# Values and decayed keys turned to tokens by 32x32 blocks on VectorE, with the blocks placed by GpSimd, in a hybrid RWKV-7 step

## The chip, the cores and the metric

The kernel runs on one core of a Trainium2 chip. A core has a matrix engine (TensorE, in the profile PE for its products and PEld for the loading of its stationary operand), VectorE (DVE), ScalarE (ACT), GpSimd (POOL), and queues that issue transfers (SP's is the one used here almost alone). Each engine works through its own list of instructions in order, and waits at the head of the list when an operand is not ready. The metric is the device time of one execution in microseconds (us). The kernel before took 2240.18 us (median of three runs, 2237.89 to 2241.36).

## What is computed

One layer of a bidirectional RWKV-7 mixer beside a gated convolution, on 384 tokens (128 of context, 256 latent) with 2048 channels in 32 heads of 64. The part that matters here is the scan, which runs in both directions d:

```python
def step(S, inp):
    r_t, w_t, k_t, v_t, a_t, b_t = inp
    sa = jnp.einsum('dbhij,dbhj->dbhi', S, a_t)
    S = S * w_t[..., None, :] + sa[..., :, None] * b_t[..., None, :] + v_t[..., :, None] * k_t[..., None, :]
    y = jnp.einsum('dbhij,dbhj->dbhi', S, r_t)
    return S, y
...
y_a = (y.astype(h.dtype) * jax.nn.silu(g_a)) @ w_out_a
...
return merged @ w_o, S_fin
```

All else is large projections: `z = h @ w_in` with 20864 columns, three output projections, and elementwise work. All is float32; the projections are computed as three products of split halves (a high part, rounded to the matrix engine's format, and the low part that is left).

## The kernel before, in words

Channels lie on the 128 partitions and tokens along a row, so that a block of 128 channels holds two heads. There are 16 blocks (`b` from 0 to 15). The scan is done in chunks of 64 tokens, `NCH` = 6 per direction.

Two kinds of work share the matrix engine, whose order is written out by hand. The first is the **stream** (`Stream`, L111): projections against weights that come in as `raw` tiles, are split into `whi` by ScalarE (L88) and `wlo` (the low part) by VectorE (L89), and are multiplied in units of three products (`mm3`, L81 to L83). `ds_.go(n)` puts n units into the engine's order. The second is the scan of the blocks, in whose gaps the units stand. Per block, in this order:

- `prep_b`: VectorE forms `bk` (L672, L673: for each chunk the 64 columns of b and the 64 columns of k, both undecayed) and `pr` (L674 to L679). Then come 14 units (`PB0`), `finish` of the block before (the matrix engine turns `ytok`, L931, after VectorE's L925, which waits for GpSimd's `rs`, L924), and for each direction the products `pA` (L700), masked into `A` by VectorE (L706), with 6 units (`PB1`) behind each. GpSimd scales `bk` by the chunk's decay (L713), as soon as the products have read it. The diagonal 32x32 corners of `A` go through memory (L710, L716) to the tile `U`, and VectorE inverts them all in a chain of 60 dependent steps (L721 and L723 in turn, in whose gaps the scheduler places other work of VectorE, such as L89). ScalarE turns the result (L727), and transfers take it back into `A` and into `x11` (L728 to L735; the profile calls that tile x).
- `prep_c`: the values `v` (and `vr`, a copy of `v` read backwards) and the scaled `bk` are turned from channels to tokens by the matrix engine, three or four 128x128 turns into a PSUM bank at a time (L761, L770), and copied out by ScalarE into the lower half of `sav` (L763) and into `bt` (L771). Then `pav` (L776) multiplies `A` with `sav`, and GpSimd clears a part of `A` (L783).
- `drive` and `go` fill up to 80 units (`WINDOW`), in which `prep_a` of the next block runs; then `scan` begins with the products `pH` (L852), which read `x11`, and goes on to `pq` (L831, reads `A` and `sav`), `pu` (L838, reads `bt`) and `po`.
- `norm`: mean, variance and scale of `ytok` (L915 to L925).

The order on VectorE, ScalarE, GpSimd and SP is the scheduler's; the order on the matrix engine is the program's own. `tmp` takes one of eight buffers in turn.

Of the kernel before, what the change touches and what calls it, by code (L numbers as in the profile page):

```python
# [9 lines left out]
F32 = mybir.dt.float32  # L10
# [5 lines left out]
P = 128  # L16
# [5 lines left out]
C = 64  # L22
NCH = 6
# [33 lines left out]
def hybrid_step(ctx, tc, cst, x_prompt, x_sample, state_f, state_b, c, c_ctx, ada_w, ada_b, norm_g,  # L57
# [3 lines left out]
    V, S, G, TE = nc.vector, nc.scalar, nc.gpsimd, nc.tensor  # L61
# [14 lines left out]
    ident = cs[:, C_ID:C_ID + P]  # L76
# [176 lines left out]
    def pcol(i, n=1):  # L253
        return par[:, i:i + n]
# [151 lines left out]
    r_, k_, v_, ga_ = {}, {}, {}, {}  # L406
    box = {}

    def tmp(nm):
        return box["sp"].tile([P, T], F32, tag="t", name=nm, bufs=8)  # L410
# [134 lines left out]
    sp = ctx_sc.enter_context(tc.tile_pool(name="sp", bufs=1))  # L545
# [6 lines left out]
    for i in range(3):  # L552
        t = tmp(f"lst_{i}")
# [4 lines left out]
    for m in range(4):  # L558
# [6 lines left out]
        t = tmp(f"lin_{m}")  # L565
# [3 lines left out]
        src = t[0:96, ::-1] if m % 2 else t[0:96, :]  # L569
# [20 lines left out]
    def bank(nm):  # L590
        return ps1.tile([P, 4, P], F32, tag="A", name=nm, bufs=5)
# [4 lines left out]
    def flat(a):  # L596
        return a.rearrange("p n t -> p (n t)")
# [4 lines left out]
    def hl_parts(t, hi, nm):  # L602
        lo = sp.tile([P, T], F32R, tag="t", name=f"lo_{nm}", bufs=8)
        S.copy(hi[:], t[:])
        V.tensor_tensor(lo[:], t[:], hi[:].bitcast(F32), ALU.subtract)
        return hi, lo
# [56 lines left out]

    def prep_b(b, o):

        r, kk = r_[b], o["kk"]
        o["pr"], o["bk"] = [], []
        for d in range(2):
            ep, em, kd, bn = o["ep"][d], o["em"][d], o["kd"][d], o["bn"][d]
            pr = sp.tile([P, NCH, P], F32, tag=f"pr{d}", name=f"pr_{b}_{d}")  # L670
            bk = sp.tile([P, NCH, P], F32, tag=f"bk{d}", name=f"bk_{b}_{d}")
# [20 lines left out]
        A = sp.tile([P, 2, 2 * NCH, P], F32, tag="A", name=f"A_{b}")  # L692
        o["A"] = A
        for d in range(2):
            pr, bk = o["pr"][d], o["bk"][d]
# [15 lines left out]

        for d in range(2):
            G.tensor_tensor(o["bk"][d][:], o["bk"][d][:], o["ep"][d][:, :, C:C + 1].broadcast_to([P, NCH, P]), ALU.mult)  # L713

        U = sp.tile([48, 32, 32], F32, tag="U", name=f"U_{b}")
        nc.sync.dma_start(U[:], ui[:].rearrange("d e i s t -> (d e i) s t"))  # L716
# [19 lines left out]

    def prep_c(b, o):

        r, v, A = r_[b], v_[b], o["A"]

        s_in = sp.tile([P, 2, C], F32, tag="s_in", name=f"s_in_{b}")
        for d in range(2):
            for h in range(2):
                for jb in range(2):
                    p0 = C * h + 32 * jb
                    nc.sync.dma_start(s_in[p0:p0 + 32, d, :].rearrange("i (b j) -> i b j", j=32),
                                      ctx_st[d][0, 0, 2 * b + h].rearrange("(b i) j -> i b j", i=32)
                                      [:, :, 32 * jb:32 * jb + 32])

        sav = sp.tile([P, 2 * NCH, P], F32, tag="sav", name=f"sav_{b}")  # L750
        bt = sp.tile([P, 2 * NCH, P], F32, tag="bt", name=f"bt_{b}")
        o["sav"], o["bkt"] = sav, bt
        for d in range(2):
            if d == 0:
                src = v
            else:
                src = tmp(f"vr_{b}")
                S.copy(src[:], v[:, ::-1])
            pv = bank(f"pv_{b}_{d}")
            for q in range(3):  # L760
                TE.transpose(pv[:, q, :], src[:, q * P:(q + 1) * P], ident)  # L761
            for e in range(2):
                S.copy(sav[C:P, NCH * d + e:NCH * d + NCH:2, :], pv[C * e:C * e + C, 0:3, :])  # L763
            yield 1
        for d in range(2):

            for n0, n1 in (((0, 4), (4, 5)), ((0, 3), (4, 6)))[d]:
                pb = bank(f"pb_{b}_{d}_{n0}")
                for n in range(n0, n1):
                    TE.transpose(pb[:, n - n0, :], o["bk"][d][:, n, :], ident)  # L770
                S.copy(bt[:, NCH * d + n0:NCH * d + n1, :], pb[:, 0:n1 - n0, :])  # L771
                yield 1
        pvs = [bank(f"pav_{b}_{d}") for d in range(2)]
        for f in range(2 * NCH):
            for h in range(2):
                TE.matmul(flat(pvs[f // NCH][hss[h]])[:, C * (f % NCH):C * (f % NCH) + C], A[C:P, 0, f, hss[h]],  # L776
                          sav[C:P, f, hss[h]], start=True, stop=True)
        for d in range(2):
            for h in range(2):
                S.copy(sav[0:C, NCH * d:NCH * d + NCH, hss[h]],  # L780
                       flat(pvs[d][hss[h]])[:, 0:NCH * C].rearrange("p (n i) -> p n i", i=C))

        G.memset(A[C:P, 0, :, :], 0.0)  # L783
        yield 2
        ks = o["kd"]
        V.tensor_tensor(ks[0][:], ks[0][:], ks[1][:, ::-1], ALU.add)
        V.scalar_tensor_tensor(ks[0][:], ks[0][:], pcol(RK + b), r[:], ALU.mult, ALU.mult)
        o["bsum"] = hl_parts(ks[0], sp.tile([P, T], F32R, tag="t", name=f"bsh_{b}", bufs=8), f"bs_{b}")
        yield 1
        for h in range(2):  # L790
            for d in range(2):
                V.transpose(st[1][hss[h], d, hss[h]], s_in[hss[h], d, :])
# [145 lines left out]
    def drive(gen, prio=0, at=None, fn=None):  # L938
        n = i = 0
        while True:  # L940
            if i == at:
                fn()
            i += 1
            with tc.high_priority(offset=prio):
                u = next(gen, None)
            if u is None:
                return n
            ds_.go(u)
            n += u
# [6 lines left out]
    for b in range(NB):  # L956
        if b < NB - 1:
            if b > 0:
                ds_.urgent += [(add_rk, b + 1), (add_gv, b)]
        if b == NB - 2:  # L960
            ds_.fills += [(add_gv, NB - 1)] + [(add_ob, g) for g in range(8)]
        pb_gen = prep_b(b, cur)
        ds_.go(next(pb_gen))
        if prev is not None:
            finish(b - 1, prev)
        drive(pb_gen)
        n = drive(prep_c(b, cur))
        nxt = {}
        if b < NB - 1:
            while f"gv{b}" not in ds_.done:  # L970
                ds_.go(1)
                n += 1
            n += drive(prep_a(b + 1, nxt))
        w = WINDOW + (FIRST if b == 0 else LAST if b == NB - 1 else 0)
        if n < w:
            ds_.go(w - n)

        def keys():

# [128 lines left out]
    for half in range(2):  # L1108
# [8 lines left out]
        for s in range(3):  # L1117
# [10 lines left out]
            if half == 1:  # L1128
                f = rsf[:, s, :]
# [37 lines left out]
```

## Time and profile before

| | |
|---|---|
| median of 3 runs | 2240.18 us |
| the profiled execution | 2242.0 us |
| its span, first to last instruction | 2240.2 us |
| mean granted clock of the matrix engine | 0.996 |
| ACT busy | 1044.3 us (47%) |
| POOL busy | 116.5 us, 113 instructions |
| GpSimd's scaling of `bk` (L713) | 32 times, 50.2 us |
| turns of `bk` on PE (L770) | 160, 27.9 us busy |
| turns of `v` and `vr` on PE (L761) | 96 |
| ScalarE's copies into `sav` behind them (L763) | 64, 30.2 us |

The blocks run from about 185 us to 1890 us; block 3, which the prediction works through, has its products `pA` at 521.67 and 526.55 us. The time of a product counts from its start to its modelled end, and the next one starts before that, so the distance between starts tells what a product takes from the engine. Times in a timeline are from the start of the span: start, duration, engine, line, operation, tiles, count, and in brackets the idle time before and what ended it.

### The profile page before, as it was taken

To read this page: it belongs to the slowest core of one execution; us is meant where nothing else is said; L and a number is where in the kernel's file an instruction comes from. 1 tells how busy PE (TensorE), PEld (TensorE's weight loads), DVE (VectorE), ACT (ScalarE), POOL (GpSimd) and SP (SyncE) were. 2 spreads that over 40 slices of the span, in tenths; PEclk is the share of its full clock that TensorE was granted. 3 is DMA by queue.
4 is the path that set the end of the run, shared out by engine and by line. 5 is a ranking of instruction groups with operands and counts; after the bars stand their busy time and mean duration, and the time that the engine had idled before them with its cause. 6 is when DMAs were issued, how large, how long until landed. Compare 5 with 4: busy or idle time off the path is not lost.

```text
span 2240.2 us, 40545 instructions
## 1 busy us (share of the span) xinstructions
PE 2179.2 (97%) x16020; PEld 2064.9 (92%) x16020; DVE 1540.2 (69%) x3208; ACT 1044.3 (47%) x1800; POOL 116.5 (5%) x113
## 2 busy tenths in 40 slices
PE   5899999999999999999999999999999999999998
PEld 3588999999999999999999999999999999998988
DVE  3248567787777778777878787777777774444354
ACT  4245445454545454454545454546455543333333
POOL 2000010101010100000010101010100000000000
PEclk9999999999999999999999999999999999999999
DMA  9973544444444445443444434444445455886633
GB/s 335 346 211 116 147 129 133 111 120 125 112 125 120 113 117 132 115 132 103 124 109 133 111 110 134 112 118 140 120 121 143 146 179 162 292 281 230 221 132 113
DMA packets 440397, 339.97 MB, mean 152 GB/s; under 512 B 95552, under 2 KB 421776, under 8 KB 439312
## 3 DMA queue, kind: packets, MB, share of 16 engines
q1 hardware_dynamic: 438720, 335.63, 51.1%
q8 instruction: 126, 2.06, 0.4%
q10 hardware_dynamic: 432, 1.57, 0.2%
q14 instruction: 63, 0.52, 0.1%
q0 software_dynamic: 1056, 0.19, 0.1%
HBM read 307.37 MB, written 29.36 MB: 150 GB/s over the span
## 4 chain that ended last, share of the span: by engine, by line
PE 81%; DVE 8%; DMA 5%; ACT 3%; SPq 2%; issue 1%; POOL 0%; POOLq 0%; ACTq 0%; DVEq 0%
PE d_rk L81 4%; PE d_rk L83 4%; PE d_rk L82 4%; PE d_gv L81 3%; PE d_gv L82 3%; PE d_gv L83 3%; DMA raw_adah<-in_ada_w_dram 3%; PE pA L700 2%; PE d_oa L81 2%; PE d_oa L83 2%; PE d_oa L82 2%; PE d_bc L81 2%; PE d_mb L81 2%; PE d_bc L83 2%; PE d_bc L82 2%; PE d_bx L81 2%
## 5 line engine op out<-in xcount | busy, mean ns | idle before, releaser
L721 DVE TENSOR_TENSOR ut<-U 48x30 f32<-48x30 f32 (+14 forms) x480 | 154.6, 322 | 16.2 <-DMA U<-ui 4.1
L81 PE MATMUL d_rk<-h_hi,whi_rk 128*128 128x384 f32 x480 | 163.0, 340 | 0.6 <-ACT lst L554 0.6
L723 DVE TENSOR_TENSOR U<-U,ut 48x30 f32<-48x30 f32 (+14 forms) x480 | 154.5, 322 | 12.1
L81 PE MATMUL d_gv<-h_hi,whi_gv 128*128 128x384 f32 x480 | 161.0, 335 | 0.0
L83 PE MATMUL d_gv<-h_hi,wlo_gv 128*128 128x384 f32 x480 | 160.7, 335 | 0.0
L82 PE MATMUL d_gv<-h_lo,whi_gv 128*128 128x384 f32 x480 | 160.7, 335 | 0.0
L83 PE MATMUL d_rk<-h_hi,wlo_rk 128*128 128x384 f32 x480 | 160.4, 334 | 0.0
L82 PE MATMUL d_rk<-h_lo,whi_rk 128*128 128x384 f32 x480 | 160.4, 334 | 0.0
L88 ACT CAST whi_gv<-raw_gv 128x1024 fp32r<-128x1024 f32 (+1 forms) x64 | 64.0, 1000 | 139.6 <-PE d_rk L82 96.9
L88 ACT CAST whi_rk<-raw_rk 128x1024 fp32r<-128x1024 f32 x60 | 63.0, 1054 | 106.4 <-PE d_rk L82 31.7
L89 DVE TENSOR_TENSOR wlo_rk<-raw_rk,whi_rk 128x1024 fp32r<-128x1024 f32 x60 | 72.9, 1218 | 44.9 <-ACT whi_rk L88 39.7
L81 PE MATMUL d_gb<-h_hi,whi_gb 128*128 128x384 f32 x256 | 92.2, 360 | 0.0
L924 POOL TENSOR_TENSOR rs<-var,nhalf 128x6 f32<-128x6 f32 x16 | 21.2, 1325 | 1364.1 <-DVE var L922 1364.1
L81 PE MATMUL d_bc<-h_hi,whi_bc 128*128 128x384 f32 x256 | 92.2, 360 | 0.0
L81 PE MATMUL d_bg<-h_hi,whi_bg 128*128 128x384 f32 x256 | 92.1, 360 | 0.0
L81 PE MATMUL d_bx<-h_hi,whi_bx 128*128 128x384 f32 x256 | 92.1, 360 | 0.0
L81 PEld LDWEIGHTS d_rk<-h_hi,whi_rk 128*128 128x128 f32 x480 | 90.1, 188 | 1.8 <-ACT lst L554 0.9
L81 PE MATMUL d_ma<-h_hi,whi_ma 128*128 128x384 f32 x256 | 91.7, 358 | 0.0
L81 PE MATMUL d_ob<-ybh,whi_ob 128*128 128x384 f32 x256 | 88.9, 347 | 2.6 <-ACT whi_ob L88 2.1
L81 PEld LDWEIGHTS d_gv<-h_hi,whi_gv 128*128 128x128 f32 x480 | 90.5, 189 | 0.2
L82 PEld LDWEIGHTS d_gv<-h_lo,whi_gv 128*128 128x128 f32 x480 | 90.5, 188 | 0.0
L83 PEld LDWEIGHTS d_gv<-h_hi,wlo_gv 128*128 128x128 f32 x480 | 90.4, 188 | 0.0
(315 smaller groups left out, 6641.9 us busy)
## 6 DMA issues: line engine op xcount, KB each, us to landing
raw_adah<-in_ada_w_dram SPq DMA_DIRECT2D x64, 512.0 KB, 8.6
raw_rk<-in_w_in_dram SPq DMA_DIRECT2D x60, 512.0 KB, 5.3
raw_gv<-in_w_in_dram SPq DMA_DIRECT2D x60, 512.0 KB, 4.9
raw_ma<-in_w_in_dram SPq DMA_DIRECT2D x16, 1024.0 KB, 5.5
raw_mb<-in_w_in_dram SPq DMA_DIRECT2D x16, 1024.0 KB, 5.7
raw_bc<-in_w_in_dram SPq DMA_DIRECT2D x16, 1024.0 KB, 5.5
raw_bx<-in_w_in_dram SPq DMA_DIRECT2D x16, 1024.0 KB, 5.4
raw_bg<-in_w_in_dram SPq DMA_DIRECT2D x16, 1024.0 KB, 5.5
```

The costliest lines, as they stand in the source:

```text
L81: TE.matmul(out, wh, xh, start=start, stop=False)
L82: TE.matmul(out, wh, xl, start=False, stop=False)
L83: TE.matmul(out, wl, xh, start=False, stop=stop)
L88: S.copy(hi[0:rows], src)
L89: V.tensor_tensor(lo[0:rows], src, hi[0:rows].bitcast(F32), ALU.subtract)
L700: TE.matmul(pas[h, n // 4 * 4][:, n % 4, :], bk[hss[h], n, :], pr[hss[h], n, :], start=True, stop=True)
L721: V.tensor_tensor(tv, U[:, 0:s, s:s + 1].broadcast_to([48, s, w]), U[:, s:s + 1, s + 1:].broadcast_to([48, s, w]), ALU.mult)
L723: V.tensor_tensor(U[:, 0:s, s + 1:], U[:, 0:s, s + 1:], tv, ALU.add)
L924: G.tensor_tensor(rs[:], var[:], nhalf[:], ALU.pow)
```

## The change

The 16 turns per block on the matrix engine, the copy `vr` and ScalarE's copies out of PSUM are gone. Instead VectorE turns each 32x32 block in place within its own 32 partitions (`V.transpose`): `v` and `v` backwards at the start of `prep_b` into two temporary tiles `vt`, and each direction's scaled `bk` in place behind GpSimd's scaling. GpSimd then copies blocks from one group of 32 partitions to another: 16 copies of 32 x 192 elements into `sav`, and 32 of the same size into `bt`. The matrix engine no longer has units between the turns; since `go` fills up to the same window, these units stand later.

```diff
     def prep_b(b, o):
 
-        r, kk = r_[b], o["kk"]
+        r, kk, v = r_[b], o["kk"], v_[b]
+
+        sav = sp.tile([P, 2 * NCH, P], F32, tag="sav", name=f"sav_{b}")
+        o["sav"] = sav
+        for d in range(2):
+            x = tmp(f"vt_{b}_{d}")
+            V.transpose(x[:], v[:, ::-1] if d else v[:])
+            x = x[:].rearrange("p (n e t) -> p n e t", e=2, t=32)
+            for e in range(2):
+                for q in range(4):
+                    G.tensor_copy(sav[C + 32 * e:C + 32 * e + 32, NCH * d:NCH * d + NCH, 32 * q:32 * q + 32],
+                                  x[32 * q:32 * q + 32, :, e, :])
...
         for d in range(2):
             G.tensor_tensor(o["bk"][d][:], o["bk"][d][:], o["ep"][d][:, :, C:C + 1].broadcast_to([P, NCH, P]), ALU.mult)
+            V.transpose(flat(o["bk"][d][:]), flat(o["bk"][d][:]))
...
     def prep_c(b, o):
...
-        for d in range(2):
-            if d == 0:
-                src = v
-            else:
-                src = tmp(f"vr_{b}")
-                S.copy(src[:], v[:, ::-1])
-            pv = bank(f"pv_{b}_{d}")
-            for q in range(3):
-                TE.transpose(pv[:, q, :], src[:, q * P:(q + 1) * P], ident)
-            for e in range(2):
-                S.copy(sav[C:P, NCH * d + e:NCH * d + NCH:2, :], pv[C * e:C * e + C, 0:3, :])
-            yield 1
-        for d in range(2):
-
-            for n0, n1 in (((0, 4), (4, 5)), ((0, 3), (4, 6)))[d]:
-                pb = bank(f"pb_{b}_{d}_{n0}")
-                for n in range(n0, n1):
-                    TE.transpose(pb[:, n - n0, :], o["bk"][d][:, n, :], ident)
-                S.copy(bt[:, NCH * d + n0:NCH * d + n1, :], pb[:, 0:n1 - n0, :])
-                yield 1
+            for p in range(4):
+                for q in range(4):
+                    G.tensor_copy(bt[32 * p:32 * p + 32, NCH * d:NCH * d + NCH, 32 * q:32 * q + 32],
+                                  o["bk"][d][32 * q:32 * q + 32, :, 32 * p:32 * p + 32])
```

Behind the change the lines of the kernel are numbered anew: `bk` is scaled at L724 (L713 before), `A` masked at L717 (L706), the chain is L733 and L735 (L721 and L723), and `rs` is L920 (L924). Two places show how the scheduler's order moves.

GpSimd's list in block 3, from the scale `rs` of block 2's output to the clearing of `A`, before:

```order
L924 TENSOR_TENSOR rs_4995<-var_4992,nhalf 128x6
L713 TENSOR_TENSOR bk_0_4999<-bk_0_4999,ep_1152 128x768
L713 TENSOR_TENSOR bk_1_5005<-bk_1_5005,ep_1154 128x768
L783 MEMSET A_5063 64x1536
```

The same list after the change:

```order
L676 COPY sav_5064<-vt_0_5065 32x6x32 x7
L920 TENSOR_TENSOR rs_5061<-var_5058,nhalf 128x6
L676 COPY sav_5064<-vt_0_5065 32x6x32
L676 COPY sav_5064<-vt_1_5075 32x6x32 x8
L724 TENSOR_TENSOR bk_0_5086<-bk_0_5086,ep_1152 128x768
L767 COPY bt_5330<-bk_0_5086 32x6x32 x15
L724 TENSOR_TENSOR bk_1_5092<-bk_1_5092,ep_1154 128x768
L767 COPY bt_5330<-bk_0_5086 32x6x32
L767 COPY bt_5330<-bk_1_5092 32x6x32 x16
L779 MEMSET A_5150 64x1536
```

Seven copies now stand ahead of `rs`, nine between it and the first scaling, and fifteen between the two scalings.

VectorE's list in block 3, from the first direction's last mask to the first steps of the chain on `U`, before:

```order
L706 TENSOR_TENSOR A_5063<-pA_0_1_4_5067,cs 128x2x2x64
L605 TENSOR_TENSOR lo_bs_5350<-kd_0_4672,bsh_5349 128x384
L89 TENSOR_TENSOR wlo_rk_0_0_5091<-raw_rk_0_5087,whi_rk_0_0_5090 128x1024
L706 TENSOR_TENSOR A_5063<-pA_1_0_0_5115,cs 128x4x2x64
L706 TENSOR_TENSOR A_5063<-pA_1_1_0_5116,cs 128x4x2x64
L706 TENSOR_TENSOR A_5063<-pA_1_0_4_5117,cs 128x2x2x64
L706 TENSOR_TENSOR A_5063<-pA_1_1_4_5118,cs 128x2x2x64
L89 TENSOR_TENSOR wlo_rk_0_1_5095<-raw_rk_0_5087,whi_rk_0_1_5094 128x1024
L89 TENSOR_TENSOR wlo_rk_1_0_5300<-raw_rk_1_5296,whi_rk_1_0_5299 128x1024
L721 TENSOR_TENSOR ut_5159<-U_5157 48x30
L723 TENSOR_TENSOR U_5157<-U_5157,ut_5159 48x30
```

After the change:

```order
L717 TENSOR_TENSOR A_5150<-pA_0_1_4_5154,cs 128x2x2x64
L89 TENSOR_TENSOR wlo_rk_0_0_5178<-raw_rk_0_5174,whi_rk_0_0_5177 128x1024
L725 STREAM_TRANSPOSE bk_0_5086<-bk_0_5086 128x768
L717 TENSOR_TENSOR A_5150<-pA_1_0_0_5202,cs 128x4x2x64
L717 TENSOR_TENSOR A_5150<-pA_1_1_0_5203,cs 128x4x2x64
L717 TENSOR_TENSOR A_5150<-pA_1_0_4_5204,cs 128x2x2x64
L717 TENSOR_TENSOR A_5150<-pA_1_1_4_5205,cs 128x2x2x64
L725 STREAM_TRANSPOSE bk_1_5092<-bk_1_5092 128x768
L89 TENSOR_TENSOR wlo_rk_0_1_5182<-raw_rk_0_5174,whi_rk_0_1_5181 128x1024
L89 TENSOR_TENSOR wlo_rk_1_0_5429<-raw_rk_1_5425,whi_rk_1_0_5428 128x1024
L733 TENSOR_TENSOR ut_5248<-U_5246 48x30
L735 TENSOR_TENSOR U_5246<-U_5246,ut_5248 48x30
```

A turn of `bk` now stands ahead of the second direction's masks, and the other ahead of two low parts and of the chain; each waits for GpSimd's scaling of that direction. The two turns of `v` stand between the subtraction of the mean (L913) and the variance (L917) of the block before. On the matrix engine the rows of L761 and L770 are gone; in the other engines' lists nothing else of this stretch moves that the prediction speaks of, but in three of the blocks (2, 6 and 10) one low part (L89) more stands inside the chain on `U` than before.

More of the change, by code (lines that the diff above doesn't have):

```diff
@@ L737, in prep_c @@
     def prep_c(b, o):
-        r, v, A = r_[b], v_[b], o["A"]
+        r, A, sav = r_[b], o["A"], o["sav"]
         s_in = sp.tile([P, 2, C], F32, tag="s_in", name=f"s_in_{b}")
@@ L748, in prep_c @@
                                       [:, :, 32 * jb:32 * jb + 32])
-        sav = sp.tile([P, 2 * NCH, P], F32, tag="sav", name=f"sav_{b}")
         bt = sp.tile([P, 2 * NCH, P], F32, tag="bt", name=f"bt_{b}")
-        o["sav"], o["bkt"] = sav, bt
+        o["bkt"] = bt
         for d in range(2):
-            if d == 0:
-                src = v
-            else:
-                src = tmp(f"vr_{b}")
-                S.copy(src[:], v[:, ::-1])
-            pv = bank(f"pv_{b}_{d}")
-            for q in range(3):
-                TE.transpose(pv[:, q, :], src[:, q * P:(q + 1) * P], ident)
-            for e in range(2):
-                S.copy(sav[C:P, NCH * d + e:NCH * d + NCH:2, :], pv[C * e:C * e + C, 0:3, :])
-            yield 1
-        for d in range(2):
-            for n0, n1 in (((0, 4), (4, 5)), ((0, 3), (4, 6)))[d]:
-                pb = bank(f"pb_{b}_{d}_{n0}")
-                for n in range(n0, n1):
-                    TE.transpose(pb[:, n - n0, :], o["bk"][d][:, n, :], ident)
-                S.copy(bt[:, NCH * d + n0:NCH * d + n1, :], pb[:, 0:n1 - n0, :])
-                yield 1
+            for p in range(4):
+                for q in range(4):
+                    G.tensor_copy(bt[32 * p:32 * p + 32, NCH * d:NCH * d + NCH, 32 * q:32 * q + 32],
+                                  o["bk"][d][32 * q:32 * q + 32, :, 32 * p:32 * p + 32])
         pvs = [bank(f"pav_{b}_{d}") for d in range(2)]
```

## The prediction

> **What bounds the kernel now.** First the page: busy time of each engine, and the chain of work that ended last by engine.
>
> ```profile
> PE 2179.2 (97%) x16020; PEld 2064.9 (92%) x16020; DVE 1540.2 (69%) x3208; ACT 1044.3 (47%) x1800; POOL 116.5 (5%) x113
> PE 81%; DVE 8%; DMA 5%; ACT 3%; SPq 2%; issue 1%; POOL 0%; POOLq 0%; ACTq 0%; DVEq 0%
> ```
>
> The matrix engine is busy nearly always and carries the chain; GpSimd is idle. So work taken from PE should be time gained, unless PE already arrives early somewhere. To see that, I read the stretch that holds the turns, and the next place where PE needs a result from outside. The turns on the chain, in order of time (block 1):
>
> ```profile
> 314.75 0.33 PE pv L761 x3
> ...
> 316.47 0.44 PE pb L770 x4
> ```
>
> A turn takes 0.11 us of the engine (0.33 / 3, 0.44 / 4). There are 6 + 10 a block: 1.76 us, and 28 us over 16 blocks. That is all PE can give.
>
> All of it stands between the products `pA` and `pH`. `pH` reads `x11`, which comes over the other branch: masks, transfer, chain on `U`, transfers. In block 3 I take the end of the chain on `U`, the last issue of the transfer into `x11`, the times to landing of this block's two such transfers, and the start of `pH`:
>
> ```profile
> 566.97 0.21 DVE L723 TENSOR_TENSOR U<-U,ut 48x30 f32<-48x30 f32 x1
> 575.78 1.06 SPq L735 DMA_DIRECT2D x<-uo  x1
> DMA to landing us min/median/max: 3.4/4.5/5.5
> 579.65 0.62 PE L852 MATMUL pH<-x,A 32*32 32x32 f32 x48
> ```
>
> PE did not wait at 579.65, so the last transfer took the 3.4: it landed at 579.2, and the spare is **0.45 us**. Block 4 and block 8 in the same way:
>
> ```profile
> 680.99 0.47 SPq L735 DMA_DIRECT2D x<-uo  x1
> DMA to landing us min/median/max: 1.8/1.9/2.0
> 686.17 0.62 PE L852 MATMUL pH<-x,A 32*32 32x32 f32 x48
> 1103.09 0.47 SPq L735 DMA_DIRECT2D x<-uo  x1
> DMA to landing us min/median/max: 1.7/1.9/2.0
> 1106.78 0.62 PE L852 MATMUL pH<-x,A 32*32 32x32 f32 x48
> ```
>
> Here the spare is 3.2 and 1.7 us; I take 2.45, their middle, for blocks of this kind. Seven blocks (3, 5, 7, 9, 11, 13, 14) are like block 3, seven (2, 4, 6, 8, 10, 12, 15) like 4 and 8. In blocks 0 and 1 the transfer lands far ahead; block 1:
>
> ```profile
> 358.15 0.92 SPq L735 DMA_DIRECT2D x<-uo  x1
> 370.20 0.62 PE L852 MATMUL pH<-x,A 32*32 32x32 f32 x48
> ```
>
> Even the longest landing above, 5.5 us, leaves 6.5 here. So, in 14 blocks, two chains of nearly one length run side by side from `pA` to `pH`. Shortening PE's alone gives little in the tight blocks, and lengthening VectorE's costs in all.
>
> **What the change does to VectorE's chain.** The prices first: GpSimd's clears of two sizes, its scaling of `bk`, VectorE's turn of 64 columns and its pass over 384.
>
> ```profile
> L579 POOL MEMSET st<- x2: 307/309/311, 147.6 to 147.9; 128x256 f32 x2
> L584 POOL MEMSET ep<- x4: 423/426/426, 148.1 to 149.2; 128x390 f32 x4
> L713 POOL TENSOR_TENSOR bk<-bk,ep x32: 1479/1498/2871, 188.1 to 1793.3; 128x768 f32<-128x768 f32 x32
> L792 DVE STREAM_TRANSPOSE st<-s_in x64: 193/230/246, 160.2 to 1773.6; 64x64 f32<-64x64 f32 x64
> L656 DVE TENSOR_SCALAR kd<-sig,par,omka x32: 452/471/478, 174.6 to 1753.4; 128x384 f32<-128x384 f32 x32
> ```
>
> *A copy of 192 elements* stands nowhere in the trace. From below: the clears grow by (426 - 309) / 134 = 0.87 ns an element, so 0.17 us with nothing fixed. From above: the scaling, two operands, 1.479 us / 768 = 1.93 ns, so 0.37 us. A copy reads one operand, so it is nearer the clears; with some fixed part I take **0.25 us**. *A turn on VectorE*: below, a pass over as many columns, 0.47 us for 384 and 0.94 for 768; above, six and twelve times the 0.246 of 64 columns, 1.5 and 3.0. The short turns carry a fixed part that a long one pays once, so I take 0.5 and 0.9. The upper ends would add 2.0 (`v`, twice) and 2.1 us (`bk`) ahead of the masks and make the chain as late as the last rival does.
>
> *Do the engines disturb each other?* Yes. These are GpSimd's first two scalings, and VectorE's work on two SBUF operands at the same moments:
>
> ```profile
> 188.09 1.48 POOL L713 TENSOR_TENSOR bk<-bk,ep 128x768 f32<-128x768 f32 x1 [38.43 <-PE pA L700]
> 194.22 2.37 POOL L713 TENSOR_TENSOR bk<-bk,ep 128x768 f32<-128x768 f32 x1 [4.65 <-issue]
> 188.51 3.28 DVE L89 TENSOR_TENSOR wlo_ma<-raw_ma,whi_ma 128x1024 fp32r<-128x1024 f32 x2
> 194.04 1.21 DVE L89 TENSOR_TENSOR wlo_mb<-raw_mb,whi_mb 128x1024 fp32r<-128x1024 f32 x1
> ```
>
> At 188 GpSimd came first, and two low parts took 3.28 us, not 2 x 1.21: VectorE lost 0.86. At 194 VectorE came first, and the scaling took 2.37, not 1.48: GpSimd lost 0.89, until 195.1, when the low part ended (195.25). So one waits for the other. The Trainium skill (SBUF — State Buffer, "Who interferes with whom") has it as a rule that speaks against this change: a VectorE instruction with two SBUF inputs and a GpSimd instruction that reads SBUF take one shared read port in turn, and the later one blocks fully. The trace agrees, with these 0.86 and 0.89 us. Without that rule the sum would be the first rival below; with it, the following. The steps on `U`, the low parts and the masks' neighbours L925, L934, L935 and L605 all read two SBUF tiles.
>
> Block 3 step by step. These are rows of before; what stands between is given in the lists of the two engines above.
>
> ```profile
> 516.44 0.56 DVE L917 TENSOR_TENSOR ytok<-ytok,mu 128x384 f32<-128x384 f32 x1
> 518.50 1.32 POOL L924 TENSOR_TENSOR rs<-var,nhalf 128x6 f32<-128x6 f32 x1 [83.70 <-DVE var L922]
> 519.85 0.56 DVE L925 TENSOR_TENSOR ytok<-ytok,rs 128x384 f32<-128x384 f32 x1 [1.50 <-POOL rs L924]
> 521.25 0.49 PE L931 MATMUL py<-cs,ytok 128*128 128x128 f32 x3
> 523.46 1.51 POOL L713 TENSOR_TENSOR bk<-bk,ep 128x768 f32<-128x768 f32 x1 [3.64 <-PE pA L700]
> 527.74 1.95 DVE L706 TENSOR_TENSOR A<-pA,cs 128x512 f32<-128x512 f32 x4 [0.65 <-PE pA L700]
> 528.34 1.49 POOL L713 TENSOR_TENSOR bk<-bk,ep 128x768 f32<-128x768 f32 x1 [3.37 <-PE pA L700]
> 536.63 1.22 DVE L89 TENSOR_TENSOR wlo_rk<-raw_rk,whi_rk 128x1024 fp32r<-128x1024 f32 x1 [4.48 <-ACT whi_rk L88]
> 537.92 0.18 DVE L721 TENSOR_TENSOR ut<-U 48x30 f32<-48x30 f32 x1
> ```
>
> 1. The first turn of `v` ends at 517.5. Seven copies later it is 519.35, and `rs` starts 0.85 late; L925 ends at 521.35, just as PE wants it (521.25). With 0.37 us a copy PE would wait 0.6.
> 2. Nine copies follow. VectorE now runs L925, a low part, L934, L605 and L935, all on two SBUF tiles, and the copies must slip between: I put their end at 526.0, not 523.0. The first scaling then ends at 527.5; the low part behind the masks waits for that and ends at 528.7, the turn of `bk` at 529.6, and only then do the second direction's masks begin: **1.8 us late**. They open the transfer to `U`, so the chain on `U` opens 1.8 late too, at 539.7.
> 3. Fifteen copies from 529.6 end at 533.4, the second scaling at 534.9, its turn at 535.7. VectorE stands idle for it from 531.5. Two low parts end at 538.1, which is before 539.7: no cost here.
> 4. The last copies start behind that turn, 17 in all. About 7 get through before 539.7; ten fall into the chain, where every step waits for the one before and a copy takes the port in each gap: 10 x 0.25 = **2.5 us**.
>
> So the chain is late by 4.3 us. At 0.17 us a copy the same steps give 1.4 (0.9 by the masks, three copies in the chain); at 0.37 they give 9.0 (masks 2.8, two low parts that end at 541.0 instead of 540.7, 16 copies in the chain, 5.9).
>
> What I cost at nothing: ScalarE's copies go, but ScalarE is 47% busy and ends no wait here. The units between the turns move behind `pav`, inside the same window. `pav` now stands six units behind `pA` and may wait for the masks, which PE's spare behind it absorbs; the clearing of `A` and `bt` are due only at `pq` and `pu`, after `pH`, and the last copy ends near 545, over 30 us before `pH`. If that cover went, `pu` would wait. The low part `wlo_rk` behind the second turn of `bk` is late too:
>
> ```profile
> 530.93 1.23 DVE L89 TENSOR_TENSOR wlo_rk<-raw_rk,whi_rk 128x1024 fp32r<-128x1024 f32 x1 [1.23 <-ACT whi_rk L88]
> 535.88 0.17 PE d_rk L81
> ```
>
> It begins at 535.7 and ends at 536.9. It is the second quarter of `d_rk`, whose first opens on PE at 535.88 and holds 8 units of three products at 0.17 us; so it is wanted at 540.0, less the 1.76 that PE is early, 538.3: hidden by 1.4 us. With dearer copies PE waits here too, but that wait only eats of the one at `pH`.
>
> **The sum.** Where VectorE's chain is later than PE, PE waits at `pH` for the lateness less the spare, whatever PE saved before; where it isn't, the saving counts up to 1.76. Tight blocks: 7 x (4.3 - 0.45) = 27. Loose ones: 7 x (4.3 - 2.45) = 13, and 3 x 1.21 for the low part that now stands inside the chain in three of them: 17. Blocks 0 and 1: 2 x -1.76 = -3.5. Together +40, against the profiled execution's 2242.0: 2282. The median of the runs is 1.8 below that execution, so **2280**.
>
> **The rivals.**
>
> *Copies slip through unseen* (faster). If the copies hardly touch VectorE, only the turns remain, 0.3 us late. Tight blocks then gain 0.15 each, loose ones and the first two 1.76: 1 + 9 x 1.76 = 17, so 2225, or 2223 for the median. For it: GpSimd is busy for 116.5 us of 2240. Against it: the 3.28 and 2.37 us.
>
> *Copies at the pace of the clears* (same). With 0.17 us the lateness is 1.4: 7 x 0.95 - 7 x 1.05 + 3.6 - 3.5 = -1, so 2241. The Trainium skill (GPSIMD Engine Reference, "Engine selection") calls one-input work on GpSimd roughly line-rate; from its 1.2 GHz that is an estimate of 0.16 us, and this sum. No run here shows it yet.
>
> *Copies at the scaling's pace* (much slower). With 0.37 us, 9.0 late: 7 x 8.55 + 7 x 6.55 + 3.6 - 3.5 = +106, so 2348, and up to 9 more from PE waiting for `rs` in 15 blocks.
>
> **How the numbers follow.** The forecast, 2255 to 2310, gets 0.52; the scaling's pace 0.20; the clears' pace 0.08; unseen copies 0.20. The range goes from 2221, which takes in the whole saving that the spares allow, to 2350; beyond it lie half of the dear copies. A measurement here tells 0.2% (4.5 us) from no change: faster 0.20, same 0.08, slower 0.72.
>
> **What would show it.** Right: PE waits at `pH` for the transfer into x, by some 4 us in blocks 3, 5, 7; the chain on `U` lasts longer than 29.3 us (537.92 to 567.18) by two or three; VectorE idles ahead of the second turn of `bk` until GpSimd. Each copy shows its price, and steps 1 and 2 show in the start of `rs` and of the second masks against `pA`. Wrong: no wait at `pH`, and steps on `U` as short as before; or a wait elsewhere, at `pu` or `py`, which would make GpSimd itself the bound.

## The result: 5.5% slower, and the profile after

The changed kernel took 2362.01 us (median of 5 runs, 2360.09 to 2364.32), the kernel before 2240.18: a ratio of 1.0546, interval 1.0531 to 1.056. The direction was forecast, the size was not: +122 us instead of +40, beyond the upper end of the range (2350).

The page of the changed kernel: the busy time of each engine, the chain that ended last by engine, and the groups of GpSimd's copies and of VectorE's turns of `bk` (line, engine, operation, tiles, count; then busy time and mean ns of one; then idle time before them and what ended it).

```profile
PE 2206.4 (94%) x15764; PEld 2067.7 (88%) x15764; DVE 1596.1 (68%) x3272; ACT 980.5 (42%) x1656; POOL 461.6 (20%) x881
PE 49%; DVE 25%; POOL 8%; DMA 7%; issue 5%; ACT 4%; SPq 1%; DVEq 0%; POOLq 0%; ACTq 0%
L676 POOL COPY sav<-vt 32x192 f32<-32x192 f32 x256 | 122.5, 478 | 1275.0 <-ACT ysq L915 736.5
L767 POOL COPY bt<-bk 32x192 f32<-32x192 f32 x512 | 213.8, 418 | 49.5 <-DVE bk L725 29.0
L725 DVE STREAM_TRANSPOSE bk<-bk 128x768 f32<-128x768 f32 x32 | 31.2, 977 | 94.4 <-POOL bk L724 94.4
```

PE has 256 instructions less and is busy for 27 us more, over a span that is 117.8 us longer. Its share of the chain fell from 81% to 49%, and VectorE's rose from 8% to 25%. The turns of `bk` took 0.98 us each, near the 0.9 that was forecast, but VectorE stood idle for 94.4 us ahead of them, all of it waiting for GpSimd's scaling. Whom PE waited for (sum, times, longest), without its first line, `pada`, which was no shorter before (22.9 us against 21.6):

```profile
PE py L927 <- DVE ytok L921: 17.3, 12, 5.5
PE pl L81 <- ACT lwh L88: 15.0, 8, 3.2
PE d_bx L81 <- DVE ga L440: 8.7, 3, 2.9
PE d_gb L81 <- DVE ga L440: 7.5, 2, 3.8
...
PE pH L848 <- DMA x<-uo: 0.2, 1, 0.2
```

Before, the first stood at 0.2 us and the other three were not there; and `pH`, where the prediction put the whole wait, shows 0.2. The second to fourth are the same lateness seen earlier: ScalarE's copy of the inverse (L739) waits for the end of the chain on `U`, and `lwh` and the activation that `ga` is made from stand behind it in ScalarE's list.

Block 3 shows where the chain is lost. GpSimd, VectorE and SP's queue in three views of the time line (start, duration, and in brackets the idle time before):

```profile
532.02 1.32 POOL L920 TENSOR_TENSOR rs<-var,nhalf 128x6 f32<-128x6 f32 x1
533.40 5.49 POOL L676 COPY sav<-vt 32x192 f32<-32x192 f32 x9
538.97 2.48 POOL L724 TENSOR_TENSOR bk<-bk,ep 128x768 f32<-128x768 f32 x1
542.53 5.68 POOL L767 COPY bt<-bk 32x192 f32<-32x192 f32 x15 [1.08 <-DVE bk L725]
548.29 1.48 POOL L724 TENSOR_TENSOR bk<-bk,ep 128x768 f32<-128x768 f32 x1
...
550.85 7.89 POOL L767 COPY bt<-bk 32x192 f32<-32x192 f32 x16 [0.67 <-DVE bk L725]
```

```profile
542.39 1.91 DVE L717 TENSOR_TENSOR A<-pA,cs 128x512 f32<-128x512 f32 x4
549.81 0.98 DVE L725 STREAM_TRANSPOSE bk<-bk 128x768 f32<-128x768 f32 x1 [5.50 <-POOL bk L724]
550.71 2.47 DVE L89 TENSOR_TENSOR wlo_rk<-raw_rk,whi_rk 128x1024 fp32r<-128x1024 f32 x2
557.76 0.24 DVE L733 TENSOR_TENSOR ut<-U 48x30 f32<-48x30 f32 x1 [4.58 <-DMA U<-ui]
```

```profile
539.02 6.13 SPq L721 DMA_DIRECT2D ui<-A  x4
551.92 0.39 SPq L104 DMA_DIRECT2D raw_gv<-in_w_in_dram  x1
552.49 0.45 SPq L728 DMA_DIRECT2D U<-ui  x1
```

The corners of `A` are on their way by 545.15, and the load of `U` that needs them is issued at 552.49. Between the two in SP's list stands a load of weights, `raw_gv`. It needs the buffer that the low part `wlo_rk` still reads; the first of the two low parts, which take 1.2 us each, ends at 551.9, and the load goes at 551.92. That low part stands behind the second turn of `bk`, the turn behind the second scaling, the scaling behind fifteen copies. The same three rows of the kernel before:

```profile
525.52 5.02 SPq L710 DMA_DIRECT2D ui<-A  x4
532.18 0.39 SPq L104 DMA_DIRECT2D raw_gv<-in_w_in_dram  x1
532.75 0.45 SPq L716 DMA_DIRECT2D U<-ui  x1
```

There the load of weights stood ahead of the load of `U` as well, and went as soon as its buffer was free too, but the low part ended at 532.15, only 0.3 us behind the landing of the last `ui`: 2.2 us from the end of the one row to the start of the last, now 7.3. It is so in all of the blocks 1 to 14, before and after: the load of weights ahead of `U` goes 0.03 us behind the end of a low part (`wlo_ma` in block 1, `wlo_rk` in the others).

The table gives these distances for all blocks: each is read as in block 3, from the rows of the same kinds, and summed over the 16 blocks (15 for the last column); the runs below the second are the experiments. The first six add up to the way from the first `pA` to `pH`; "chain" goes from the start of its first step to the end of its last, with whatever VectorE does in between. "Half clock" is the span times what the mean granted clock of the run lacks of 1.

| run | median us | `pA` to last `ui` landed | to issue of `U` | to chain | chain | to `x11` landed | to `pH` | `pH` to next `pA` | half clock |
|---|---|---|---|---|---|---|---|---|---|
| before | 2240.2 | 180.7 | 12.4 | 79.6 | 474.2 | 165.3 | 46.2 | 706.9 | 9 |
| changed | 2362.0 | 212.8 | 78.3 | 84.9 | 492.0 | 155.0 | 33.0 | 727.9 | 50 |
| turns_only | 2241.1 | 196.7 | 6.8 | 82.2 | 485.0 | 154.8 | 32.3 | 711.1 | 20 |
| turn_low | 2320.3 | 212.7 | 3.2 | 103.2 | 504.9 | 155.4 | 33.2 | 728.8 | 39 |
| rs_first | 2374.2 | 237.1 | 83.0 | 85.8 | 491.4 | 154.0 | 36.6 | 709.9 | 62 |
| late_rs | 2257.4 | 186.1 | 16.6 | 82.9 | 484.1 | 155.3 | 46.9 | 711.3 | 20 |
| only_v | 2273.9 | 190.8 | 10.7 | 75.4 | 491.9 | 167.9 | 27.2 | 734.5 | 25 |
| only_bk | 2322.0 | 186.6 | 83.3 | 82.1 | 494.9 | 172.7 | 12.1 | 712.1 | 35 |
| bk_late | 2263.7 | 184.0 | 11.0 | 76.8 | 497.1 | 174.4 | 28.8 | 714.4 | 18 |
| act | 2354.8 | 226.7 | 47.4 | 108.0 | 499.4 | 155.9 | 30.6 | 710.8 | 52 |
| free | 2229.8 | 185.6 | 5.9 | 87.0 | 484.7 | 156.3 | 29.4 | 707.3 | 9 |

Of the 118 us between the first `pA` and the last `pH`, 66 are the wait of `U`'s load for the load of weights, 32 late masks, 21 stand between `pH` and the next `pA` (PE's waits at `py` are 17.3), 8 are the chain together with the way from it to `x11`, and 5 the transfer into `U`; 13 came out of the spare. The chain and the way behind it are read together, since both move in `free` too, which has no copy at all: there the one is 10.5 us longer, with more of VectorE's other work between its steps, and the other 9.0 us shorter. The steps of the chain themselves took 316.8 us instead of 309.1 in the changed kernel.

### The profile page after: what moved, and what is told of

Read it like the earlier page. It is cut to its first block, busy times and chain, and to the rows that moved or that the text cites. A ratio compares the mean times of both kernels' runs of the same rounds, so it can differ in the third digit from the quotient of the medians.

```text
span 2358.0 us, 40762 instructions
## 1 busy us (share of the span) xinstructions
PE 2206.4 (94%) x15764; PEld 2067.7 (88%) x15764; DVE 1596.1 (68%) x3272; ACT 980.5 (42%) x1656; POOL 461.6 (20%) x881
## 3 DMA queue, kind: packets, MB, share of 16 engines
q8 instruction: 124, 2.03, 0.4%
## 4 chain that ended last, share of the span: by engine, by line
PE 49%; DVE 25%; POOL 8%; DMA 7%; issue 5%; ACT 4%; SPq 1%; DVEq 0%; POOLq 0%; ACTq 0%
POOL sav L676 4%; DVE ut L733 4%; DVE U L735 4%; DMA raw_adah<-in_ada_w_dram 3%; DMA U<-ui 2%; POOL bt L767 2%; PE d_oa L81 2%; PE d_oa L83 2%; PE d_oa L82 2%; DVE wlo_gv L89 2%; POOL bk L724 2%; PE d_ob L81 1%; PE d_ob L83 1%; PE acc L81 1%; PE acc L83 1%
## 5 line engine op out<-in xcount | busy, mean ns | idle before, releaser
L676 POOL COPY sav<-vt 32x192 f32<-32x192 f32 x256 | 122.5, 478 | 1275.0 <-ACT ysq L915 736.5
L767 POOL COPY bt<-bk 32x192 f32<-32x192 f32 x512 | 213.8, 418 | 49.5 <-DVE bk L725 29.0
L733 DVE TENSOR_TENSOR ut<-U 48x30 f32<-48x30 f32 (+14 forms) x480 | 158.7, 331 | 61.4 <-DMA U<-ui 49.6
L81 PE MATMUL d_rk<-h_hi,whi_rk 128*128 128x384 f32 x480 | 161.2, 336 | 10.5 <-DVE bc L467 5.0
L735 DVE TENSOR_TENSOR U<-U,ut 48x30 f32<-48x30 f32 (+14 forms) x480 | 158.1, 329 | 11.8
L83 PEld LDWEIGHTS d_rk<-h_hi,wlo_rk 128*128 128x128 f32 x480 | 90.1, 188 | 8.4 <-DVE wlo_rk L89 8.4
L725 DVE STREAM_TRANSPOSE bk<-bk 128x768 f32<-128x768 f32 x32 | 31.2, 977 | 94.4 <-POOL bk L724 94.4
L81 PE MATMUL d_mb<-h_hi,whi_mb 128*128 128x384 f32 x256 | 90.2, 352 | 3.3 <-DVE ga L440 2.9
```

Source lines behind the costliest of these rows:

```text
L81: TE.matmul(out, wh, xh, start=start, stop=False)
L83: TE.matmul(out, wl, xh, start=False, stop=stop)
L676: G.tensor_copy(sav[C + 32 * e:C + 32 * e + 32, NCH * d:NCH * d + NCH, 32 * q:32 * q + 32], x[32 * q:32 * q + 32, :, e, :])
L725: V.transpose(flat(o["bk"][d][:]), flat(o["bk"][d][:]))
L733: V.tensor_tensor(tv, U[:, 0:s, s:s + 1].broadcast_to([48, s, w]), U[:, s:s + 1, s + 1:].broadcast_to([48, s, w]), ALU.mult)
L735: V.tensor_tensor(U[:, 0:s, s + 1:], U[:, 0:s, s + 1:], tv, ALU.add)
```

## The experiments

Each ran beside the kernel before (medians 2238.4 to 2239.8 us), timed in three rounds. A fence called diff shows the edit against the changed kernel, unless it says otherwise.

**1. One part alone.** `only_v` keeps the part on `v` and turns `bk` on PE as before; `only_bk` the other way round. Their diffs are the halves of the diff above.

> Only the values are turned by blocks (two turns on VectorE, 16 copies on GpSimd per block); bk is turned on PE as before. Theory Q (the transfer into U is held on SP's queue, behind a load of weights whose buffer is freed by a low part that now stands behind the second turn of bk): without turns of bk on VectorE the load into U follows its ui transfers within about 1 us as in the kernel before, pA to the first step on U stays within 1.5 us of the 16.3 before, and only the late rs is left, the 21 us that the changed kernel lost between pH and the next pA: 2250 to 2272 us. Rival P (every copy costs, by its price of 0.34 us or more and by the port): a third of the copies, so a third of the 122 us: 2280 us, with U late by 2 us a block.

> Only bk is turned by blocks (two turns on VectorE, 32 copies on GpSimd per block); the values are turned on PE as before. Theory Q: the load into U is still held by 4 to 6 us in the 13 or 14 blocks in which a load of raw_gv or raw_rk stands ahead of it, and no wait at py is left: 2305 to 2340 us. Rival P: two thirds of the 122 us, 2320 us, with U on time and a chain on U that is some 3 us longer than 29.4 us.

Measured 2273.93 us (ratio 1.0151, 1.0134 to 1.0168) and 2322.03 us (1.0369, 1.0354 to 1.0384). The parts add up: 35 + 84 = 119 of 122 us. `only_bk` by itself says little, since both theories put it near 2320 by their size; the table tells them apart: the issue of `U` is late by 71 us in sum (83.3 against 12.4), and nothing is lost at `py`. The chain is longer too, by 21 us, 1.3 a block where rival P had some 3; but its steps took only 4 us more (313.5 instead of 309.1), and the rest is other work of VectorE between them. PE's longest wait in the blocks is then at `pav`, for ScalarE's copies of the values (20.0 us), and here `pH` does wait for the transfer into `x11`, nine times and 7.9 us in all. `only_v` came out 2 us above its range: `U` is on time, and `pH` to the next `pA` costs 27.6.

**2. One order on VectorE.** The second turn of `bk` behind the low part that frees the raw tile.

```diff
         lo = pool.tile(shape, F32R, tag=tl, name=f"{tl}_{nm}")
         S.copy(hi[0:rows], src)
-        V.tensor_tensor(lo[0:rows], src, hi[0:rows].bitcast(F32), ALU.subtract)
+        low.append(V.tensor_tensor(lo[0:rows], src, hi[0:rows].bitcast(F32), ALU.subtract).ins)
...
-            V.transpose(flat(o["bk"][d][:]), flat(o["bk"][d][:]))
+            with tc.issue_after(low[-d]):
+                V.transpose(flat(o["bk"][d][:]), flat(o["bk"][d][:]))
```

> The changed kernel with one order changed on VectorE: the second turn of bk stands behind the low part that frees the raw tile (and the first behind the one before it, where it stood already). Theory Q: the load into U is issued within 1 us of the landing of its ui transfers (6 us in the changed kernel), pA to the first step on U falls from 22.9 to 17.5 to 18.5 us, and 5 us in each of 14 blocks come back, less what the last 16 copies now cost inside the chain (up to 2 us a block): 2285 to 2320 us. Rival P: the copies are the same in number and price, so 2350 to 2370 us.

2320.25 us (1.0359, 1.0344 to 1.0374): 42 us come back from the place of one instruction a block; work and copies are the same. (For the first turn `low[-0]` is the first low part of the whole kernel, which binds nothing: that turn stays where it was.) Block 3 of this run, SP's queue and VectorE:

```profile
533.36 6.13 SPq L723 DMA_DIRECT2D ui<-A  x4
539.83 0.39 SPq L106 DMA_DIRECT2D raw_gv<-in_w_in_dram  x1
540.86 0.31 SPq L731 DMA_DIRECT2D U<-ui  x1
```

```profile
538.57 1.24 DVE L91 TENSOR_TENSOR wlo_rk<-raw_rk,whi_rk 128x1024 fp32r<-128x1024 f32 x1
545.05 0.98 DVE L728 STREAM_TRANSPOSE bk<-bk 128x768 f32<-128x768 f32 x1 [5.25 <-POOL bk L726]
545.95 1.18 DVE L91 TENSOR_TENSOR wlo_rk<-raw_rk,whi_rk 128x1024 fp32r<-128x1024 f32 x1
547.05 0.33 DVE L736 TENSOR_TENSOR ut<-U 48x30 f32<-48x30 f32 x1
547.41 0.35 DVE L738 TENSOR_TENSOR U<-U,ut 48x30 f32<-48x30 f32 x1
```

The first low part now ends at 539.81, ahead of the turn, the load of weights goes at 539.83, and the load of `U` leaves 1.4 us behind the last `ui`; in the table its wait falls from 78.3 to 3.2. Not all of the 75 us return: the turn still stands ahead of the chain on VectorE and waits 5.25 us for the scaling (18 more from the issue of `U` to the chain), and most of the last sixteen copies now fall into the chain, whose first steps take 0.33 and 0.35 us where they took 0.18 before (13 more in the chain).

**3. The turns without the copies.** GpSimd clears `bt` and the lower half of `sav` to a constant instead of copying, so the values and decayed keys are missing from the result; the turns stay where they are.

> The changed kernel without its 48 copies a block: the turns stand on VectorE in the same places as in the changed kernel, and GpSimd clears the lower half of sav and bt to a constant instead (two clears a block), so the values and the decayed keys are left out of the result. Theory Q (GpSimd's list is the bound: the copies ahead of rs and of the two scalings make these late, and the turns pass that on to VectorE and SP): with the scalings on time the turns cost next to nothing, no wait at py, U issued within 2 us of its ui transfers: 2228 to 2245 us. Rival T (the turns themselves, which stand ahead of masks and low parts, are the cost): 30 us or more above 2240, 2270 us and later.

2241.11 us, ratio 1.0008 (0.9998 to 1.0018): no difference from the kernel before. VectorE's list has the same turns in the same places; the scalings are on time, and VectorE isn't idle ahead of a single turn of `bk`. At `py` PE waits 3.3 us, where the expectation had no wait. The turns delay the last `ui` by 16 us in sum, 1 a block, and the spare and PE's saving pay for it. What costs is GpSimd's list, whose copies stand ahead of `rs` and of the scalings.

**4. PE's saving by itself.** The kernel before without its turns, filled by clears, which leaves the same values out.

```diff
-        (the turns of v, vr and bk on PE, and ScalarE's copies of them)
+        G.memset(sav[C:P], 0.25)
+        G.memset(bt[:], 0.25)
```

> The kernel before without the 16 turns a block on PE, the copy vr and ScalarE's copies behind them; the lower half of sav and bt are cleared to a constant by GpSimd instead, so the values and the decayed keys are left out of the result. Theory S (PE's saving counts only up to the spare at pH): 7 blocks x 0.45, 9 x 1.76 us, 19 us: 2219 to 2226 us. Rival F (all that PE saves is gained): 28 us, 2210 to 2214 us. Rival N (nothing of it is gained, since pH waits anyway): 2236 to 2242 us.

2229.75 us (0.9963, 0.9951 to 0.9975): 9 of PE's 28 us reach the end, half of what the spares allowed, and the time lies between the ranges of S and N. Against this run the turns on VectorE alone (run 3) cost 11 us. So as far as this run can stand for it, no placing of the copies could have won much more than 0.4% at this window.

**5. `rs` first.** GpSimd's copies into `sav` queued behind `rs`.

```diff
-        G.tensor_tensor(rs[:], var[:], nhalf[:], ALU.pow)
+        box["rs"] = G.tensor_tensor(rs[:], var[:], nhalf[:], ALU.pow).ins
...
+            with ExitStack() as behind:
+                if b:
+                    behind.enter_context(tc.issue_after(box["rs"]))
...
```

> The changed kernel with one order changed on GpSimd: rs stands ahead of all 16 copies into sav instead of behind 7 to 14 of them. Theory Q: PE's wait at py (17.3 us in 12 blocks) goes, pH to the next pA comes back from 727.9 us in sum to within 5 us of 706.9, and the stretch pA to pH is no shorter: 2338 to 2348 us. Rival P (the port and the price, wherever the copies stand): L921 and the low part behind it now run beside copies, and what is gained at py is lost again at the masks: 2355 to 2365 us.

2374.19 us (1.0599, 1.0583 to 1.0615), slower than the changed kernel by 12 us, and outside both ranges. The wait at `py` is gone, as expected (709.9 from `pH` to the next `pA`). But the copies, now all between `rs` and the first scaling, took 9.29 us for sixteen in block 3, the scaling began at 544.48, and the way to the last `ui` grew by 24 us in sum. GpSimd's list is full from `rs` to the second scaling; what is moved ahead there makes the rest late, and the rest stands on the longer path.

**6. Everything at other places.** `late_rs`: as 5, and both turns of `bk` queued behind the last step of the chain, with the copies into `bt` behind them. `late_rs_w83` and `before_w83`: this kernel and the kernel before with three units more in the window.

```diff
-            V.tensor_tensor(U[:, 0:s, s + 1:], U[:, 0:s, s + 1:], tv, ALU.add)
+            o["last"] = V.tensor_tensor(U[:, 0:s, s + 1:], U[:, 0:s, s + 1:], tv, ALU.add).ins
...
         for d in range(2):
+            with tc.issue_after(o["last"]):
+                V.transpose(flat(o["bk"][d][:]), flat(o["bk"][d][:]))
             for p in range(4):
...
-    PRO, WINDOW, FIRST, LAST = 32, 80, 24, 16
+    PRO, WINDOW, FIRST, LAST = 32, 83, 24, 16
```

> All copies and turns of the changed kernel, at other places: rs ahead of the copies into sav, both turns of bk behind the last step of the chain on U, so that 32 copies run between the chain and pu. Theory Q: no turn stands ahead of masks, low parts or the chain; the load into U follows its ui transfers within 1 us, the chain takes 29.4 to 30.5 us, no wait at py: within 10 us of the kernel without any turns (2229.75), 2228 to 2245 us. Rival P: 48 copies of 0.34 us and more still hold the port for 16 us and more a block, against VectorE's work behind the chain: 2290 to 2350 us. Rival D: bt comes too late for pu, 2250 to 2290 us with PE waiting at pu for GpSimd.

> The kernel late_rs with the window between pA and pH lengthened from 80 to 83 units (1.6 us of PE's work moved ahead of pH in each block and taken from behind the last one). Theory S (PE's saving is lost in waits between pA and pH, since the chain on U is as long as before): the window holds the saving, and 10 to 20 us of the 28 come back: 2212 to 2228 us, faster than the kernel before. Rival N: within 4 us of late_rs, since the waits sit in ScalarE's and VectorE's lists and move with the units.

> The kernel before with the window lengthened from 80 to 83 units and nothing else. PE is busy 97% and waits nowhere between pA and pH, so a later pH moves work and saves none: 2234 to 2246 us by both theories. If it comes out below 2230 us, the gain of the run with 83 units above is not the turns' doing.

`late_rs` took 2257.4 us (1.0086, 1.0071 to 1.0101). The same 48 copies and four turns cost 19 us here and 122 in the changed kernel: 103 us are their place. That is above the range of theory Q by 12, and in the range of rival D; but D's wait isn't there: at `pu` PE waits 4.8 us, all of it for ScalarE, and 4.4 before. In block 3 the 32 copies take 16.46 us, 0.51 each, beside VectorE's work ahead of `pH`, some of which is slower than before:

```profile
568.56 16.46 POOL L771 COPY bt<-bk 32x192 f32<-32x192 f32 x32 [33.18 <-DVE bk L768]
```

```profile
573.30 0.94 DVE L424 SCALAR_TENSOR_TENSOR v<-zs,par,v 128x127 f32<-128x127 f32 x2
574.17 0.69 DVE L605 TENSOR_TENSOR lo_sq<-sq,sqh 128x384 fp32r<-128x384 f32 x1
574.78 0.56 DVE L89 TENSOR_TENSOR lwl<-lraw,lwh 96x256 fp32r<-96x256 f32 x1
```

(0.74, 0.55 and 0.42 in the kernel before), and PE waits 14.4 us in all for `lwl`. How much of the 19 us this is, and how much the half clock, was not separated. The longer window didn't settle what it was meant to: the kernel before got slower by it, 2257.36 us (1.0083, 1.0066 to 1.01), which neither theory expected, and `late_rs_w83` took 2252.18 (1.006, 1.0045 to 1.0075), 5 us less than `late_rs` and outside both expectations. The three units move every load and cast against the blocks, so these two runs say only that no gain is to be had in this way.

`bk_late` moves only the part on `bk` behind the chain, and turns `v` on PE.

> Only bk is turned by blocks, both turns behind the last step of the chain on U, the 32 copies between the chain and pu; the values are turned on PE as before. Theory Q: nothing stands ahead of rs, the scalings, masks, low parts or the transfer into U, so the only costs left are the port behind the chain and PE's saving of 10 turns a block (18 us) that is mostly lost in waits, as in the kernel without turns: 2232 to 2250 us. Rival P: 32 copies of 0.4 us a block still cost two thirds of what they cost in late_rs or more: 2255 us and later.

2263.65 us (1.0109, 1.0094 to 1.0124), no better than `late_rs`, and in the range of rival P. P's cause isn't shown by that: a third fewer copies cost no less. The copies stand behind the chain, and its steps are as short as before (308.5 us in sum), yet the chain is 23 us longer, with more of VectorE's other work between the steps, and the way behind it 9; PE then waits 6.5 us at `pH`, 8.3 for `lwl` and 7.7 at `pav` for ScalarE's copies of the values. How much of the 24 us the copies make stays open.

**7. The copies on ScalarE**, everything else as changed.

```diff
-                    G.tensor_copy(sav[...
+                    S.copy(sav[...
...
-                    G.tensor_copy(bt[...
+                    S.copy(bt[...
```

> The changed kernel with its 48 copies a block on ScalarE instead of GpSimd, everything else as it is. Theory Q: rs and the scalings are on time, U is issued within 2 us of its ui transfers; ScalarE, 41% busy and without the copies out of PSUM, takes the copies between its casts, which come 1 to 3 us late in places: 2240 to 2275 us. Rival P (48 copies of 0.3 us or more are too dear wherever they stand): ScalarE's list becomes the bound ahead of whi and pav, 2300 us and later.

2354.84 us (1.0521, 1.0503 to 1.0538): theory Q's number was wrong, and rival P's fits. The price of a copy, in this run on ScalarE and in the changed kernel on GpSimd (minimum, median, maximum):

```profile
L767 ACT COPY bt<-bk x512: 346/349/357, 194.1 to 1922.9; 32x192 f32<-32x192 f32 x171
```

```profile
L767 POOL COPY bt<-bk x512: 332/341/2030, 194.6 to 1934.1; 32x192 f32<-32x192 f32 x171
```

ScalarE's price is the same and never moves, so a third engine isn't disturbed by VectorE, while a copy of GpSimd's is held for up to 2.03 us. But 48 x 0.35 = 17 us a block in ScalarE's list make its casts late, the low parts wait for these, `raw_gv` for the low part, and the load of `U` is held again (47.4 in the table, and the masks 46 us later in sum than before). It is the same hold with another engine at its head.

**8. Work for PE in its waits.** Products that nobody reads, into a free quarter of a PSUM bank: ahead of `py` behind blocks 4 and 8, and ahead of the first `pl` in six windows.

```diff
+            for _ in range(20 if m == 0 and b % 2 and 3 <= b <= 13 else 0):
+                TE.matmul(pl[:, 3, :], ident, ident, start=True, stop=True)
             pl = flat(pl[:, 0:3, :])
...
         py = bank(f"py_{b}")
+        for _ in range(38 if b in (4, 8) else 0):
+            TE.matmul(py[:, 3, :], ident, ident, start=True, stop=True)
```

> The changed kernel with products added on PE that nobody reads, into a free part of a PSUM bank, in eight of its waits: 38 ahead of py behind blocks 4 and 8 (waits of 5.5 us), 20 ahead of the first pl in six windows (waits of 1.6 to 3.2 us). PE has more to do. Theory H (a wait of PE that fills over half of a stretch of 3.41 us is followed by 3.41 us or more at half the granted clock, 1.71 us lost each time, about 41 us between 185 and 1970 us of the changed kernel): these stretches disappear behind the eight places, 10 or so, and 10 to 17 us come back: 2343 to 2354 us. Rival (the granted clock has nothing to do with the waits, or the lost time is hidden by the chain anyway): 2358 us or later.

2352.22 us (1.0507, 1.0492 to 1.0523), 10 us less than the changed kernel, with intervals that don't overlap, and with more to do; the column "half clock" would have 28 for it instead of 50. Four microseconds each (length, then busy time and count of PE, PEld, DVE, ACT, POOL, then PE's granted clock, DMA's share and GB/s) around `py` behind block 4, in the changed kernel:

```profile
762.00:766.00 4.00, 0.00 (x0) 0.00 (x0) 0.56 (x1) 0.00 (x0) 3.65 (x8) 0.88 0.87 236
766.00:770.00 4.00, 3.86 (x28) 3.33 (x29) 2.24 (x5) 1.07 (x2) 0.54 (x2) 0.50 0.02 4
770.00:774.00 4.00, 4.00 (x18) 3.85 (x18) 3.14 (x5) 1.04 (x1) 1.48 (x1) 0.77 0.37 84
```

and with the products in the wait:

```profile
762.00:766.00 4.00, 4.00 (x38) 4.00 (x37) 0.56 (x1) 0.00 (x0) 1.39 (x3) 1.00 0.10 16
766.00:770.00 4.00, 4.00 (x40) 3.71 (x39) 2.85 (x6) 2.12 (x3) 1.86 (x1) 1.00 0.12 43
```

In the changed kernel PE comes back from its wait at half its clock; with its time filled it keeps the full one. Each of the products became two instructions, so they outlasted the wait (8.65 us at `py`), and the time still fell.

## Why the prediction was wrong, step by step

- **Step 3 failed**: "Two low parts end at 538.1, which is before 539.7: no cost here." It asked who on VectorE and PE waits for these low parts, and left out SP's queue. The first of them frees the buffer for `raw_gv`, and the load of `U` stands behind that load. By the step's own numbers that low part ends at 536.9, `U` is issued at 537.5 instead of 532.75, and the chain opens 4.7 us late, not 1.8; some 40 us more, in 14 blocks. Measured, the hold grew by 66 us in sum, and the run that moved one turn took it away (12.4 before, 78.3 changed, 3.2).
- **Where PE waits** was wrong with it: the sum put all of the wait at `pH`, which shows 0.2 us. PE came late to `pH` itself, having waited before for `py`, `lwh` and `ga`, so only 13 us of the 46 us of spare were used.
- **The price of a copy** was mis-sized: 0.25 us was taken, 0.33 is the least that the rows show, and 0.42 and 0.48 are the means with what VectorE takes from it. It makes the second scaling, and so the hold, later. The upper end (0.37) was exceeded because it left out that a copy can be held.
- **Step 1** had the mechanism but only block 3's order. There seven copies stand ahead of `rs` and PE waits 1.03 us at `py`; in the blocks behind 4 and 8 there are fourteen, and it waits 5.46. The sum over all is 21 us, which was costed at nothing. (Seven copies of 0.25 us behind 517.5 end at 519.25, not 519.35; that changes nothing.)
- **Step 2 held**: the second masks begin 542.39 - 534.53 = 7.9 us behind `pA`, 6.1 before: 1.8 late. Over all blocks the `ui` transfers land 32 us later in sum, 2.0 a block.
- **Step 4** was too dear: the steps of the chain took 8 us more in sum, 0.5 a block instead of 2.5. It opened so late that most copies were done, and even where some fourteen of them ran beside it (7.2 of 8.15 us, block 3 of `turn_low`), the chain took 30.82 us instead of 29.27: 0.11 a copy, not 0.25. More of VectorE's other work came to stand between the steps than one low part in blocks 2, 6 and 10 (the whole chain is 18 us longer), but the way behind the chain is 10 us shorter.
- **The spares** were right to bound PE's saving, and too generous: without turns 9 us were gained, not 19.
- **The rival of dear copies** (2348, or 2346 with the 1.8 us that the forecast took off) came nearest in its number, by another way: it put 5.9 of its 9.0 us into the chain.
- **Missing**: PE's clock behind a wait. PE lost about 50 us to the half clock, 9 before. Not all of it adds to the time, since a slower PE that is waited for by nobody only arrives later at the next wait; the 10 us of `warm` are what eight places gave back.

## What to carry to other kernels

When an instruction becomes late, follow each thing that it releases: the buffer too, and the load that wants this buffer, and everything behind that load in an in-order queue of transfers. Before work goes to an idle engine, look at what short, urgent instructions stand in its list: GpSimd was 5% busy, but its three were those that all others waited for, and place, not amount, made 103 of 122 us. And a wait of the matrix engine can cost more than its length.

## What was not expected of the hardware

The granted clock falls to half behind waits that are quite short. PE in the changed kernel, ahead of and behind a wait (in brackets) in block 3, and the clock there:

```profile
587.20 0.34 PE L83 MATMUL pl<-l_hi,lwl 96*128 96x384 f32 x1
590.46 0.44 PE L81 MATMUL d_bx<-h_hi,whi_bx 128*128 128x384 f32 x1 [2.92 <-DVE ga L440]
...
592.13 0.52 PE L81 MATMUL d_bx<-h_hi,whi_bx 128*128 128x384 f32 x1
592.45 0.52 PE L82 MATMUL d_bx<-h_lo,whi_bx 128*128 128x384 f32 x1
```

```profile
590.00:592.00 2.00, 1.54 (x6) 1.55 (x7) 1.62 (x3) 2.00 (x4) 0.00 (x0) 0.74 0.76 143
592.00:594.00 2.00, 2.00 (x8) 2.00 (x7) 2.00 (x7) 1.81 (x6) 0.00 (x0) 0.50 1.03 334
```

The distance between two products' starts goes from 0.18 us to 0.32. Between the first `pA` and the last `pH` the half-clock stretches of the changed kernel last 3.41 us or twice that (474.90 to 478.32, or 707.01 to 713.84) and begin on one grid of 3.41 us; one follows where PE stood idle for more than about half of one stretch of the grid. Over the whole run, with 1.76 us of idle time or more in a stretch one always followed; with 1.4 to 1.7 us one began two times out of twelve; with less, none began. So the wait of 1.90 us ahead of 474.94 us led to one, and one of the same 2.9 us as above, ahead of 1507.43, to none, since it fell across two stretches (1.20 and 1.70 us). The Trainium skill (TensorE: Matmul & The Clock Gate, "HAM oscillation — how this bites in real kernels") warns of idle gaps above some 3.4 us; here 1.9 us could be enough, and the measurement decides.

The Trainium skill's rule on the shared port (SBUF — State Buffer, "Who interferes with whom") holds in its direction: sixteen copies alone would take 16 x 0.34 = 5.5 us, and took 7.89 and 8.15 beside VectorE. But it was GpSimd that lost most, not VectorE's chain: the 768 copies took 336 us where 0.34 each would be 261, and the steps of the chain 8 us more than before. What the Trainium skill calls roughly line-rate (GPSIMD Engine Reference, "Engine selection") was not reached by these copies: 0.33 us at the least for 192 elements, where the estimate by it was 0.16.
